# Which PSUM banks an output projection takes, and which engine scales its norms, in a one-core hybrid encoder layer

## The chip, the core and the metric

The kernel runs on one core of one Trainium2 chip. The metric is the device time of one execution in microseconds (us), lower is better. The kernel before took 1556.27 us in the median of three runs (1555.42 to 1558.12). One more execution was taken with the hardware profiler: it took 1553.82 us, of which 1551.8 us are the profiled span.

Five engines work side by side, each through its own list of instructions in order: TensorE (PE, matmuls and transposes, with its weight loads as PEld), VectorE (DVE), ScalarE (ACT), GpSimd (POOL), and SyncE (SP), which issues the DMAs. Matmuls write to PSUM, which this program uses as eight banks of 128x512 float32; DVE and ACT read results out of it, which is called eviction here.

## The reference

One encoder layer on 1024 tokens of width 1024: a mixer (windowed attention beside a gated delta rule) with an output projection, a cross-attention into 256 memory tokens with an output projection, and a SwiGLU feed-forward block. Each is normalised before and after:

```python
def _rms_norm(x, gain):
    y = xf * lax.rsqrt(jnp.mean(xf * xf, axis=-1, keepdims=True) + EPS)
    return y * gain

for l in range(DEPTH):
    ...
    mix = jnp.concatenate([attn_o, dn_o], axis=-1) @ w_out[l]
    x = x + _rms_norm(mix, g_mix_post[l])
    c = _memory_cross_attention(_rms_norm(x, g_cross_pre[l]), _rms_norm(mem, g_mem[l]),
                                w_cq[l], w_ckv[l], w_co[l])
    x = x + _rms_norm(c, g_cross_post[l])
    f = _swiglu(_rms_norm(x, g_ffn_pre[l]), w_gate_up[l], w_down[l])
    x = x + _rms_norm(f, g_ffn_post[l])

# inside the windowed attention, per head and block of 128 queries
denom = jnp.sum(p, axis=-1, keepdims=True) + jnp.exp(sk - m)
o = jnp.einsum('bnhgqk,bnkhd->bnqhgd', p / denom, vw)
```

## The kernel before

Every large product is made of three matmuls on operands split in a high and a low part: `split` (L103 and L104) casts the high part on ACT and subtracts the low part on DVE, or on POOL where the call says so. Weights come through `load_w` (L126): a DMA into `wraw`, then `whi` and `wlo`. Each of these three has two buffers, so the weights of a step can be made ready only when those of two steps earlier have been used.

The program is written in the order of the layer; a scheduler then interleaves the instructions on every engine, with data, buffers and banks as its limits. The stages the change touches, in the order of time:

- **Windows** (`window`, L643 to L690). Sixteen blocks of windowed attention, numbered 0 to 15. PE makes the scores (`psw`, L654), DVE masks them and takes the maximum (L656), ACT makes the exponentials (L663), and the four probability tiles are scaled by one over the sum (L671 to L674): by DVE for the first eight blocks, by ACT for the last eight. PE then transposes them (`ptw`, L680), they are split into `ph` and `pl`, and PE makes the output (`pow`, L685). The last blocks run beside the memory's value projection (`pcv`, L965).
- **Mixer projection** (`mid_gemm` with `w_out`). It works on 512 tokens at a time, here called the first and the second half, and on each in two chunks of 512 output columns. A chunk has four accumulators `pmg` (L1052), one per 128 tokens, and four weight steps; a step gives each accumulator six matmuls. So a chunk is 96 matmuls, and its first accumulator is complete 18 matmuls before its last. An eviction is a square with its sum on ACT (L1055) and a multiplication by the gain on DVE (L1056). Then each 128 tokens get: a reciprocal root on POOL (L1064, L1065), the residual on DVE (L1066), a store, a square on ACT (L1069), a second reciprocal root on POOL (L161, L162), and the scaling of the next norm into `xr` on DVE (L1072). PE turns `xr` (`ptn`).
- **Cross queries** (`cross_q`, `pcq`, L261), with the low parts of the weights made by POOL.
- **Cross-attention** (`cross_attention`). For each half four heads follow one another: 24 score matmuls (`pcs`, L1133), maximum on DVE, exponentials on ACT (L1140), sums and scaling on DVE, eight transposes (`pct`, L1149), their split into `cph` and `cpl`, 12 output matmuls (`pco`, L1159), whose result is split back into the query's tiles. `pcs` and `pco` share the pool `px` of two banks.
- **Cross projection**: `mid_gemm` with `w_co` on the first half, the transposes of its norm (`ptn`, L1190) with POOL making low parts, `mid_gemm` on the second half, and the start of the feed-forward block (`pA`, L1227).

In this part PSUM is three pools: `pg` with four banks, `pn` and `px` with two each. A pool hands out its banks in turn, in the order in which the program is written. The argument `banks` of `mid_gemm` says from which pool each accumulator of the first and of the second chunk comes. By default the second chunk takes its first two accumulators from `px` and its last two from `pg`. In the program `mid_gemm` on the first half of the cross projection stands behind all heads of both halves, so its turn in `px` comes after all of their tiles.

Of the kernel before, what the change touches and what calls it, by code (L numbers as in the profile page):

```python
# [13 lines left out]
AF = mybir.ActivationFunctionType  # L14
ALU = mybir.AluOpType
# [8 lines left out]
NT = S // P  # L24
# [52 lines left out]
def tile_hybrid_block(  # L77
# [6 lines left out]
    nc = tc.nc  # L84
    x, mem, out = x[0], mem[0], out[0]
    w_in, w_out, w_cq, w_ckv, w_co = w_in[0], w_out[0], w_cq[0], w_ckv[0], w_co[0]
# [100 lines left out]
    d_x1 = dram.tile([S, D], F32, name="d_x1")  # L187
    d_x2 = dram.tile([S, D], F32, name="d_x2")
# [443 lines left out]
    def window(n, g):  # L632

        tok = slice(n * P, (n + 1) * P)
        k0, k1 = max(n - 1, 0), min(n + 1, NT - 1) + 1
        nb = k1 - k0
        w = nb * P
        band = C[:, _AT["band0"] - C0 + (k0 - n + 1) * P:][:, 0:w]

        khi, klo = (t[:, k0 * P:k1 * P] for t in keys[g])  # L640
        qr = tw.tile([P, 4, P], F32, tag="qr", name="qr", bufs=1)
        for r in range(2):
            nc.sync.dma_start(qr[64 * r:64 * r + 64], d_q[256 * g:256 * g + 256, tok].rearrange("(h e) t -> e h t", h=4))  # L643
        qs = tw.tile([P, 4, P], F32R, tag="qs", name="qs")
        nc.scalar.copy(qs, qr)
        nc.gpsimd.tensor_tensor(qs[64:128], qr[64:128], f32(qs[64:128]), ALU.subtract)

        m4 = tw.tile([P, 4], F32, tag="m4", name="m4")
        ssum = tw.tile([P, 4], F32, tag="ssum", name="ssum")
        pr = []  # L650
        for hh in range(4):
            pp = pw.tile([P, 512], F32, tag="pw", name="psw")
            for i, kk in enumerate((khi, klo)):
                nc.tensor.matmul(pp[:, 0:w], qs[:, hh, :], kk, start=(i == 0), stop=(i == 1))  # L654
            sc = tw.tile([P, 384], F32, tag="sc", name="sc", bufs=8)
            nc.vector.tensor_tensor_reduce(out=sc[:, 0:w], in0=pp[:, 0:w], in1=band, scale=0.125,  # L656
                                           scalar=sink[:, 4 * g + hh:4 * g + hh + 1], op0=ALU.add, op1=ALU.max,
                                           accum_out=m4[:, hh:hh + 1])
            pr.append(sc)
        nm = tw.tile([P, 4], F32, tag="nm", name="nm")  # L660
        nc.vector.tensor_scalar(nm, m4, -1.0, None, ALU.mult)
        for hh in range(4):
            nc.scalar.activation(pr[hh][:, 0:w], pr[hh][:, 0:w], AF.Exp, bias=nm[:, hh:hh + 1],  # L663
                                 accum_out=ssum[:, hh:hh + 1])
        es = tw.tile([P, 4], F32, tag="es", name="es")
        nc.gpsimd.tensor_tensor(es, sink[:, 4 * g:4 * g + 4], m4, ALU.subtract)
        nc.scalar.activation(es, es, AF.Exp)
        nc.vector.tensor_tensor(es, es, ssum, ALU.add)
        nc.vector.reciprocal(es, es)
        for hh in range(4):  # L670
            if g * NT + n < 8:  # L671
                nc.vector.tensor_scalar(pr[hh][:, 0:w], pr[hh][:, 0:w], es[:, hh:hh + 1], None, ALU.mult)
            else:
                nc.scalar.mul(pr[hh][:, 0:w], pr[hh][:, 0:w], es[:, hh:hh + 1])  # L674
        yield
        po = pw.tile([P, 4, P], F32, tag="pow", name="pow", bufs=1)
        for j in range(nb):
            pp = pw.tile([P, 512], F32, tag="pw", name="ptw")
            for hh in range(4):
                nc.tensor.transpose(pp[:, hh * P:(hh + 1) * P], pr[hh][:, j * P:(j + 1) * P], ident)  # L680
            ph = tw.tile([P, 512], F32R, tag="ph", name="ph")
            pl = tw.tile([P, 512], F32R, tag="pl", name="pl")
            split(ph, pl, pp)
            for i, pe_ in enumerate((ph, pl)):
                nc.tensor.matmul(po.rearrange("p h t -> p (h t)"), vhl[:, k0 + j, g].rearrange("p r e -> p (r e)"), pe_,  # L685
                                 start=(j == 0 and i == 0), stop=(j == nb - 1 and i == 1))
        ao = tw.tile([P, 4, P], F32, tag="ao", name="ao", bufs=1)[0:64]
        nc.scalar.copy(ao, po[64:128])
        nc.vector.tensor_tensor(ao, po[0:64], ao, ALU.add)
        nc.sync.dma_start(d_mix[g * 256:(g + 1) * 256, tok].rearrange("(h e) t -> e h t", e=64), ao)  # L690
# [322 lines left out]
    def turn_norm(xn, gname, his, los, pin=False):  # L1013

        for k in range(KT):
            pt = pn.tile([P, 512], F32, tag="pn", name="ptn")
            for j in range(4):
                t = nc.tensor.transpose(pt[:, j * P:(j + 1) * P], xn[j][:, k * P:(k + 1) * P], ident)
                if pin and k + j == 0:
                    tc.keep_in_program_order(t)  # L1020
            split(his[:, k, :], los[:, k, :], pt, gain(gname, k))
# [9 lines left out]

    PG, PN, PX = (pg, "pg"), (pn, "pn"), (px, "px")

    def mid_gemm(tz, act, w, gp, res, dst, hf, between=None, banks=([PG] * 4, [PX] * 2 + [PG] * 2)):


        zs = [tz.tile([P, D], F32, tag="z", name="z", bufs=4) for _ in range(4)]
        sss = [tz.tile([P, 2], F32, tag="zss", name="zss", bufs=8) for _ in range(4)]
        for ch in range(2):
            cs = slice(ch * 512, (ch + 1) * 512)  # L1040
            if ch and between:
                between()

            pp = [q_.tile([P, 512], F32, tag=t_, name="pmg") for q_, t_ in banks[ch]]
            for kp in range(4):
                whi, wlo = load_w(w[kp * 256:(kp + 1) * 256, cs], 2, 512)
                for t in range(4):
                    tt = slice(t * P, (t + 1) * P)
                    for kk in range(2):
                        k = 2 * kp + kk  # L1050
                        for i, (w_, a) in enumerate(((whi, 0), (whi, 1), (wlo, 0))):
                            nc.tensor.matmul(pp[t], act[a][:, k, tt], w_[:, kk, :], start=(k == 0 and i == 0),  # L1052
                                             stop=(k == KT - 1 and i == 2))
            for t in range(4):
                nc.scalar.activation(zs[t][:, cs], pp[t], AF.Square, accum_out=sss[t][:, ch:ch + 1])  # L1055
                nc.vector.tensor_tensor(zs[t][:, cs], pp[t], gp[:, cs], ALU.mult)  # L1056
        xn = []
        for t in range(4):
            tok = slice(hf * HALF + t * P, hf * HALF + (t + 1) * P)
            z = zs[t]  # L1060
            xr = tz.tile([P, D], F32, tag="xr", name="xr", bufs=XR)
            nc.sync.dma_start(xr, res[tok, :])
            rs = tz.tile([P, 1], F32, tag="prs", name="prs", bufs=4)
            nc.gpsimd.tensor_scalar(rs, sss[t][:, 1:2], sss[t][:, 0:1], D * EPS, ALU.add, ALU.add)  # L1064
            nc.gpsimd.tensor_tensor(rs, rs, mhalf[:, 0:1], ALU.pow)  # L1065
            nc.vector.scalar_tensor_tensor(z, z, rs, xr, ALU.mult, ALU.add)  # L1066
            nc.sync.dma_start(dst[tok, :], z)
            s2 = tz.tile([P, 1], F32, tag="ps2", name="ps2", bufs=4)
            nc.scalar.activation(xr, z, AF.Square, accum_out=s2)  # L1069
            r2 = tz.tile([P, 1], F32, tag="pr2", name="pr2", bufs=4)  # L1070
            rstd_of(r2, s2, 1.0 / D, EPS)
            nc.vector.tensor_scalar(xr, z, r2, None, ALU.mult)  # L1072
            xn.append(xr)
        return xn

# [6 lines left out]
    tz = L1.enter_context(pool("tz", 1))  # L1082
    gp = gpost_tile(tz, g_mix_post)
    mxT = [operand(opA, "s0"), [opB_first[0], opB3.tile([P, KT, HALF], F32R, tag="b3", name="b3")]]
# [7 lines left out]
                              .rearrange("(k p) t -> p k t", p=P))  # L1092
            split(mxT[hf][0][:, k2, :], mxT[hf][1][:, k2, :], raw[:, k2, :])
    LR.close()
    xn0 = mid_gemm(tz, mxT[0], w_out, gp, x, d_x1, 0, banks=([PG] * 4, [PX] * 2 + [PN] * 2))
    h2T = [[opB.tile([P, KT, HALF], F32R, tag=b1, name=b1), opB_first[2]]]
    xn1 = mid_gemm(tz, mxT[1], w_out, gp, x, d_x1, 1, between=lambda: turn_norm(xn0, "cross", *h2T[0], pin=True))
    h2T.append(operand(opA, "s0"))
    turn_norm(xn1, "cross", *h2T[1])

# [64 lines left out]
    q1 = cross_q(1)  # L1165
# [10 lines left out]
    tz = L3.enter_context(pool("tz2", 1, side="right"))  # L1176
# [16 lines left out]
    for k in range(KT):  # L1193
        pt = turned_k(xn, k)
        nc.scalar.activation(raw[:, k, :], pt, AF.Identity, scale=gain("ffn", k))
        split(x1h[:, k, :], x1l[:, k, :], raw[:, k, :], eng=nc.gpsimd)
    xn = mid_gemm(tz, q1, w_co, gp, d_x1, d_x2, 1)
    T2, T4 = (blocks(t) for t in operand(opB, "s1"))
    T1, T3 = (blocks(t) for t in operand(opB, "s2"))
    for k in range(HK):  # L1200
# [355 lines left out]
```

## Time and profile before

| | |
|---|---|
| median of three runs | 1556.27 us |
| profiled execution | 1553.82 us |
| its span | 1551.8 us |
| PE busy | 1488.0 us (96%) |
| DVE busy | 1074.3 us (69%) |
| ACT busy | 740.3 us (48%) |
| POOL busy | 379.9 us (24%) |
| PE's share of the chain that ended last | 70% |

Places in time (us from the start of the span): the last windows run until about 572, the mixer projection from 552 to 647, the queries and the first half's heads from 647 on, the first half's cross projection begins at 762, the second half's heads end at 839, the second half's cross projection ends at 903, and the feed-forward block fills the rest.

In the rows of a timeline or of the chain the first number is the start, the second the duration, then engine, line, operation, output and inputs, and the count of merged instructions; in square brackets stands how long the engine sat idle before it, and who released it. Matmuls overlap one another, so the pace of a long merged row says more than the duration of one matmul.

### The profile page before, as it was taken

What the parts mean: (1) busy time and instruction counts of PE and PEld (TensorE: products, weight loads), DVE (VectorE), ACT (ScalarE), POOL (GpSimd) and SP (SyncE); (2) the same over time, 40 slices, a digit from 0 to 9 for tenths busy, and PEclk for the clock granted to TensorE, in tenths of its full rate; (3) what the DMA queues carried; (4) which work ended last, traced back from release to release, by engine and by line L of the source; (5) the groups of instructions that cost most, each with busy time, mean ns of one, the idle gap of its engine ahead of it and who ended that gap; (6) DMA issues with size and microseconds to landing.
All of it is one profiled execution on the core that took longest, in us unless ns stands there. A gap on an engine that the chain in (4) does not pass through costs nothing.

```text
span 1551.8 us, 21044 instructions
## 1 busy us (share of the span) xinstructions
PE 1488.0 (96%) x7451; PEld 1248.9 (80%) x7451; DVE 1074.3 (69%) x1728; ACT 740.3 (48%) x1522; POOL 379.9 (24%) x364
## 2 busy tenths in 40 slices
PE   6999999998999999999987999999999999999997
PEld 5888888787989788888876887888888888888786
DVE  6868999686888766643444577776867554696665
ACT  5578732557467764443333664332323332354532
POOL 2020210111256103433000531443433432000021
PEclk9999999999999999999999999999999999999999
DMA  6244575856996755542210554344433334853354
GB/s 205 75 117 136 158 189 158 190 173 187 328 303 210 246 196 180 179 155 77 68 41 27 188 192 144 116 128 129 156 118 113 105 106 150 290 188 98 102 175 164
DMA packets 264710, 242.95 MB, mean 157 GB/s; under 512 B 33800, under 2 KB 203677, under 8 KB 264605
## 3 DMA queue, kind: packets, MB, share of 16 engines
q1 hardware_dynamic: 264605, 241.62, 50.0%
q8 instruction: 58, 0.95, 0.3%
q14 instruction: 47, 0.39, 0.1%
HBM read 172.07 MB, written 66.88 MB: 154 GB/s over the span
## 4 chain that ended last, share of the span: by engine, by line
PE 70%; DVE 7%; DMA 5%; ACT 5%; issue 2%; SPq 1%; POOL 1%; DVEq 0%; POOLq 0%; ACTq 0%
PE pmg L1052 11%; PE pD L1227 8%; PE pE L1227 8%; PE pA L1227 7%; PE pdX L1417 6%; PE pcq L261 5%; PE pdA L1417 4%; PE pB L1227 4%; PE psc L809 3%; PE pg L261 3%; PE pdD L1417 2%; PE pco L1159 2%; PE pcs L1133 2%; PE pck L949 1%; PE pdX L1510 1%
## 5 line engine op out<-in xcount | busy, mean ns | idle before, releaser
L103 ACT CAST whi<-wraw 128x1024 fp32r<-128x1024 f32 x108 | 113.6, 1052 | 176.6 <-PE pmg L1052 50.1
L261 PE MATMUL pg<-hlo,whi 128*128 128x512 f32 x352 | 139.7, 397 | 0.0
L261 PE MATMUL pg<-hhi,whi 128*128 128x512 f32 x352 | 139.3, 396 | 0.0
L261 PE MATMUL pg<-hhi,wlo 128*128 128x512 f32 x352 | 138.8, 395 | 0.0
L104 POOL TENSOR_TENSOR wlo<-wraw,whi 128x1024 fp32r<-128x1024 f32 x38 | 92.5, 2435 | 184.1 <-ACT whi L103 176.6
L104 DVE TENSOR_TENSOR wlo<-wraw,whi 128x1024 fp32r<-128x1024 f32 x70 | 87.1, 1245 | 71.9 <-ACT whi L103 64.4
L1052 PE MATMUL pmg<-whi,b 128*128 128x512 f32 x384 | 117.0, 393 | 1.1 <-DVE b L104 0.9
L1227 PE MATMUL pA<-s,whi 128*128 128x512 f32 x352 | 109.3, 392 | 1.0 <-ACT m L1244 1.0
L1052 PEld LDWEIGHTS pmg<-whi,b 128*128 128x128 f32 x384 | 71.5, 188 | 16.3 <-DVE b L104 1.4
L261 PEld LDWEIGHTS pg<-hhi,whi 128*128 128x128 f32 x352 | 66.6, 189 | 13.6 <-ACT hhi L103 0.2
L1417 PE MATMUL pdX<-dhl,whi 128*128 128x512 f32 x264 | 76.0, 390 | 1.5 <-DVE zv L1472 0.7
L1227 PEld LDWEIGHTS pA<-s,whi 128*128 128x128 f32 x352 | 65.5, 188 | 14.7 <-ACT m L1244 1.5
L261 PEld LDWEIGHTS pg<-hhi,wlo 128*128 128x128 f32 x352 | 66.5, 189 | 13.0
L261 PEld LDWEIGHTS pg<-hlo,whi 128*128 128x128 f32 x352 | 66.5, 189 | 12.9
L1304 POOL TENSOR_TENSOR act<-act,up 128x512 f32<-128x512 f32 x33 | 50.1, 1519 | 87.6 <-DVE up L1303 47.3
L1052 PE MATMUL pmg<-wlo,b 128*128 128x512 f32 x192 | 71.1, 391 | 0.0
L103 ACT CAST whi<-araw 128x1024 fp32r<-128x1024 f32 (+1 forms) x36 | 35.4, 982 | 71.0 <-PE pdX L1417 27.6
L1227 PE MATMUL pA<-s,wlo 128*128 128x512 f32 x176 | 68.7, 391 | 0.0
L104 DVE TENSOR_TENSOR wlo<-araw,whi 128x1024 fp32r<-128x1024 f32 (+1 forms) x36 | 40.8, 1133 | 38.9 <-ACT whi L103 38.9
L286 DVE SCALAR_TENSOR_TENSOR acc<-cp,cols,acc 128x1024 f32<-128x1024 f32 x48 | 62.1, 1295 | 0.1
L1276 POOL TENSOR_TENSOR sr<-wraw 128x512 f32<-128x512 f32 x22 | 31.0, 1410 | 126.5 <-DMA wraw<-in_w_gate_up_dram 125.2
L1447 POOL TENSOR_SCALAR frs<-sq 128x1 f32<-128x1 f32 x8 | 12.0, 1498 | 195.9 <-ACT jk L1436 194.9
(414 smaller groups left out, 4107.8 us busy)
## 6 DMA issues: line engine op xcount, KB each, us to landing
wraw<-in_w_gate_up_dram SPq DMA_DIRECT2D x52, 512.0 KB, 3.8
kv<-d_kv SPq DMA_DIRECT2D x32, 512.0 KB, 6.7
wraw<-in_w_in_dram SPq DMA_DIRECT2D x22, 512.0 KB, 4.7
b<-in_w_down_dram SPq DMA_DIRECT2D x20, 512.0 KB, 6.9
araw<-d_as SPq DMA_DIRECT2D x20, 512.0 KB, 3.7
pz<-d_pz SPq DMA_DIRECT2D x32, 256.0 KB, 5.2
wraw<-in_w_ckv_dram SPq DMA_DIRECT2D x16, 512.0 KB, 9.2
wraw<-in_w_out_dram SPq DMA_DIRECT2D x16, 512.0 KB, 3.7
```

The lines of the kernel that those rows point to most:

```text
L103: nc.scalar.copy(hi, src)
L104: (eng or nc.vector).tensor_tensor(lo, src, f32(hi), ALU.subtract)
L261: nc.tensor.matmul(p_, w[:, k, :], ah[a][:, k, :], start=(k == 0 and i == 0), stop=(k == nk - 1 and i == 2))
L286: nc.vector.scalar_tensor_tensor(acc, cp[:, t:t + S], taps[t], acc, ALU.mult, ALU.add)
L809: nc.tensor.matmul(out[:, d, h, :], lt[:, d, h, :], rt[:, d, h, :], start=True, stop=True)
L1052: nc.tensor.matmul(pp[t], act[a][:, k, tt], w_[:, kk, :], start=(k == 0 and i == 0), stop=(k == KT - 1 and i == 2))
L1133: nc.tensor.matmul(pp[:, t2_, :], q[a][:, ct, tt], kr_[b_][:, ct, :], start=(j == 0 and i == 0), stop=(j == 1 and i == 2))
L1159: nc.tensor.matmul(po, vr_[a][:, kt, cs], pts[kt][b_], start=(kt == 0 and i == 0), stop=(kt == 1 and i == 2))
L1227: nc.tensor.matmul(out_, w[a][:, k, :], xx[b_][:, k, :], start=(start and k == 0 and i == 0), stop=(k == HK - 1 and i == 2), skip_group_ch ...
L1276: nc.gpsimd.tensor_tensor(s[0], b_[:, 0:HK], b_[:, HK:], ALU.add)
L1304: nc.gpsimd.tensor_tensor(o_, o_, up, ALU.mult)
L1417: nc.tensor.matmul(banks[t], a[:, k - k0, tt], w, start=(first and k == 0 and i == 0), stop=(k == NB - 1 and i == 2), skip_group_check=not ...
```

## The change

Three edits.

1. The default of `banks` becomes four accumulators from `pg` in both chunks. The two calls of the mixer projection name their banks, the same ones as before. So the two calls of the cross projection alone take other banks: `px` is out of their second chunk.
2. A new argument `vec` says which engine scales the norm. DVE does it, as before, in the mixer's first half and the cross projection's second half. In the mixer's second half and the cross projection's first half ACT does it, as an Identity activation with the reciprocal root as scale.
3. The windows' probabilities are scaled by DVE in blocks 0 to 7 and 13 to 15, by ACT in blocks 8 to 12.

```diff
-            if g * NT + n < 8:
+            if not 8 <= g * NT + n < 13:
                 nc.vector.tensor_scalar(pr[hh][:, 0:w], pr[hh][:, 0:w], es[:, hh:hh + 1], None, ALU.mult)
             else:
                 nc.scalar.mul(pr[hh][:, 0:w], pr[hh][:, 0:w], es[:, hh:hh + 1])
...
-    def mid_gemm(tz, act, w, gp, res, dst, hf, between=None, banks=([PG] * 4, [PX] * 2 + [PG] * 2)):
+    def mid_gemm(tz, act, w, gp, res, dst, hf, between=None, banks=([PG] * 4, [PG] * 4), vec=False):
...
-            nc.vector.tensor_scalar(xr, z, r2, None, ALU.mult)
+            if vec:
+                nc.vector.tensor_scalar(xr, z, r2, None, ALU.mult)
+            else:
+                nc.scalar.activation(xr, z, AF.Identity, scale=r2)
...
-    xn0 = mid_gemm(tz, mxT[0], w_out, gp, x, d_x1, 0, banks=([PG] * 4, [PX] * 2 + [PN] * 2))
+    xn0 = mid_gemm(tz, mxT[0], w_out, gp, x, d_x1, 0, banks=([PG] * 4, [PX] * 2 + [PN] * 2), vec=True)
...
-    xn1 = mid_gemm(tz, mxT[1], w_out, gp, x, d_x1, 1, between=lambda: turn_norm(xn0, "cross", *h2T[0], pin=True))
+    xn1 = mid_gemm(tz, mxT[1], w_out, gp, x, d_x1, 1, banks=([PG] * 4, [PX] * 2 + [PG] * 2),
+                   between=lambda: turn_norm(xn0, "cross", *h2T[0], pin=True))
...
-    xn = mid_gemm(tz, q1, w_co, gp, d_x1, d_x2, 1)
+    xn = mid_gemm(tz, q1, w_co, gp, d_x1, d_x2, 1, vec=True)
```

Lines after L1072 move by up to four in the changed kernel: `pcs` is L1137 there, `pct` L1153, `pco` L1163.

The scheduler answers with another order. On PE, in the second head of the second half, this stood before (`kr` and `vr` are the memory's keys and values, `b_7540` and `b_7541` the second half's query tiles, into which the heads' results go back):

```order
L1133 MATMUL pcs<-kr_6142,b_7540 128x256
L1149 MATMUL pct<-ident,cpr 128x128 x8
L1159 MATMUL pco<-cph,vr_6143 128x512 x2
L1159 MATMUL pco<-cpl,vr_6143 128x512
L1159 MATMUL pco<-cph,vr_6144 128x512
```

The last score matmul, the transposes and the outputs followed one another, with nothing else between, and so in the third and the fourth head. In the changed kernel PE has this at the second head's outputs (`b_6962` and `b_6963` are the first half's query tiles):

```order
L1052 MATMUL pmg<-wlo,b_6962 128x512
L1052 MATMUL pmg<-whi,b_7540 128x512
L1052 MATMUL pmg<-whi,b_7541 128x512
L1052 MATMUL pmg<-wlo,b_7540 128x512
L1052 MATMUL pmg<-whi,b_7540 128x512
L1052 MATMUL pmg<-whi,b_7541 128x512
L1163 MATMUL pco<-cph,vr_6143 128x512 x2
L1052 MATMUL pmg<-wlo,b_7540 128x512
L1163 MATMUL pco<-cpl,vr_6143 128x512
L1163 MATMUL pco<-cph,vr_6144 128x512
```

Projection matmuls moved in among the heads, those of the first half and then of the second. In that head 32 of them stand between scores and transposes, 21 between transposes and outputs, 22 behind the outputs. In the third head it is 1 between the two halves of the scores, 19 ahead of the transposes, none between transposes and outputs and 4 behind. In the fourth head 10 stand between the halves of the scores, 10 ahead of the transposes and none between transposes and outputs; then follow four transposes of the first half's norm and 120 projection matmuls mixed with the other transposes. From the end of the second half's projection on PE's order is that of before.

On ACT, from the casts of the second head's results to the fourth head's exponentials, this stood before:

```order
L103 CAST b_7540<-pco 128x512 x2
L1140 ACTIVATE cpr,csum<-pcs,cmx 128x256 x4
L103 CAST cph<-pct 128x512 x2
L103 CAST b_7540<-pco 128x512 x2
L1140 ACTIVATE cpr,csum<-pcs,cmx 128x256 x4
```

The changed kernel has, from the casts of the second head's results on:

```order
L103 CAST b_7540<-pco 128x512 x2
L1075 ACTIVATE xr<-z,pr_8429 128x1024
L1075 ACTIVATE xr<-z,pr_8442 128x1024
L1069 ACTIVATE xr,ps_8453<-z 128x1024
L103 CAST whi<-wraw 128x1024
L1075 ACTIVATE xr<-z,pr_8455 128x1024
L1144 ACTIVATE cpr,csum<-pcs,cmx 128x256 x4
L103 CAST whi<-wraw 128x1024
L103 CAST cph<-pct 128x512 x2
```

Three scalings, a square and a weight cast of the projection moved ahead of the third head's exponentials.

On DVE, in the norm of the mixer's second half (the `pr` are the reciprocal roots, `b_6963` the low part of a query):

```order
 L1056 TENSOR_TENSOR z<-pmg,gpost 128x512
-L1072 TENSOR_SCALAR xr<-z,pr_6845 128x1024
 L1066 SCALAR_TENSOR_TENSOR z<-z,prs,xr 128x1024
-L1072 TENSOR_SCALAR xr<-z,pr_6858 128x1024
-L1072 TENSOR_SCALAR xr<-z,pr_6871 128x1024
-L104 TENSOR_TENSOR b_6963<-pcq,b_6962 128x512
-L1072 TENSOR_SCALAR xr<-z,pr_6884 128x1024
-L104 TENSOR_TENSOR b_6963<-pcq,b_6962 128x512
+L104 TENSOR_TENSOR b_6963<-pcq,b_6962 128x512 x3
```

The four scalings left DVE; they stand on ACT now, between its squares and weight casts.

## The prediction

> **What bounds the kernel now.** The page comes first: how much of the span has PE at work.
>
> ```profile
> span 1551.8 us, 21044 instructions
> ## 1 busy us (share of the span) xinstructions
> PE 1488.0 (96%) x7451; PEld 1248.9 (80%) x7451; DVE 1074.3 (69%) x1728; ACT 740.3 (48%) x1522; POOL 379.9 (24%) x364
> ```
>
> PE is busy for 96%, and the change takes no matmul away. So it can gain only where PE stands still or is stretched, 64 us at least. The next view is the table of windows, 10 us each; its columns are the window, its length, the busy us of PE, PEld, DVE, ACT and POOL with their counts, PE's granted clock, the DMA share and GB/s.
>
> ```profile
> 790.00:800.00 10.00, 10.00 (x49) 8.22 (x48) 6.62 (x11) 5.36 (x15) 0.00 (x0) 1.00 0.14 52
> 800.00:810.00 10.00, 6.34 (x39) 4.93 (x39) 4.89 (x11) 4.11 (x12) 0.00 (x0) 0.94 0.00 0
> 810.00:820.00 10.00, 7.39 (x40) 6.02 (x39) 4.55 (x10) 3.19 (x11) 0.00 (x0) 0.89 0.01 2
> 820.00:830.00 10.00, 7.80 (x37) 5.82 (x36) 3.92 (x7) 2.15 (x4) 0.00 (x0) 0.83 0.00 0
> 830.00:840.00 10.00, 6.12 (x31) 4.19 (x30) 5.31 (x12) 4.19 (x12) 0.00 (x0) 1.00 0.00 0
> 840.00:850.00 10.00, 10.00 (x46) 8.28 (x45) 2.45 (x2) 2.11 (x2) 0.00 (x0) 1.00 0.24 82
> ```
>
> From 800 to 840 no engine is full, DMA rests, and PE's clock drops with its idleness. The chain that ended last, in order of time, shows what runs there (a row is a merged piece of the chain).
>
> ```profile
> 712.13 2.79 PE pco L1159 x12
> ...
> 766.52 2.87 PE pcs L1133 x24
> 769.39 6.60 PE pmg L1052 x29
> 776.87 3.64 PE pmg L1052 x16
> ...
> 802.31 3.14 PE pcs L1133 x24
> 809.64 3.79 PE pco L1159 x10
> 814.81 3.14 PE pcs L1133 x24
> 822.15 4.24 PE pco L1159 x10
> 827.77 3.15 PE pcs L1133 x24
> 839.38 26.80 PE pmg L1052 x117
> ```
>
> These are the second half's second, third and fourth head, each waiting for itself: scores, maximum, exponentials, transposes, outputs, split. Earlier heads had query or projection matmuls between their steps; these have none. Two banks explain it. Projection chunk two has its first two accumulators in `px`, whose turn comes after the last head, so only its other two could go ahead; with two weight buffers that stops after two steps. The rest of the projection waits until 839.38.
>
> **Edit 1, the banks.** PE's own timeline gives the end of the first head's outputs, and the steps of the fourth head.
>
> ```profile
> 800.98 0.40 PE L1159 MATMUL pco<-cph,vr 128*128 128x512 f32 x1
> ...
> 834.03 0.63 PE L1149 MATMUL pct<-ident,cpr 128*128 128x128 f32 x4 [0.80 <-DVE cpr L1143]
> ...
> 838.04 0.40 PE L1159 MATMUL pco<-cph,vr 128*128 128x512 f32 x1
> ```
>
> The stretch runs from 800.98 + 0.40 = 801.38 to 839.38, 38.0 us. Where PE had cover, a head cost 2.87 (24 scores), 776.87 - 769.39 - 6.60 = 0.88 (eight transposes) and 2.79 (12 outputs), 6.54 us; three heads cost 19.6. So 18.4 us are PE time in which projection matmuls could run, at 26.80 / 117 = 0.229 us each. In the new order they do. What stays, by the counts of the order:
>
> - The second head has 32, 21 and 22 of them behind its three steps, 7.3, 4.8 and 5.0 us. A filled step of before had 6.60 us and less. Nothing is left there.
> - The third and fourth head have nothing between transposes and outputs. In the trace this pair took 838.44 - 834.03 = 4.41 us for 0.44 + 2.79 of work: 1.2 left in each, 2.4.
> - The fourth head has ten (2.3 us) ahead of its transposes. Unfilled, the second transposes came 834.03 - (827.77 + 3.15) = 3.1 us after the scores: 0.8 left.
> - Behind the last outputs the projection reads the head just made. That took 839.38 - 838.44 = 0.94 us; four transposes now cover 0.44 of it, 0.5 left. Behind the third head four matmuls read it too, but its first column block first: I take 0.5 again.
> - ACT has five passes of 1.06 us (a row below) ahead of the third head's exponentials, 5.3 us, and a POOL reciprocal root to wait for; PE has 22 projection and 24 score matmuls, 7.9 us, over it. I take 1.0, between 0 and 2.5 (one POOL step of 1.47 and one pass more).
>
> Together 5.2 us left, a gain of 13.2. The bounds: 16.0 if only the 2.4 is left; 9.1 if the fourth head, the least covered, kept its whole excess of 839.38 - 827.77 - 6.54 = 5.1, with 1.2, 0.5 and 2.5 for the rest.
>
> Do four banks cost more elsewhere? The rows of the two eviction lines, and of two ACT and POOL operations (count, then minimum, median and maximum in ns):
>
> ```profile
> L1055 ACT ACTIVATE z<-pmg x32: 581/598/623, 574.5 to 903.9; 128x512 f32<-128x512 f32 x32
> L1056 DVE TENSOR_TENSOR z<-pmg,gpost x32: 676/692/693, 575.2 to 906.1; 128x512 f32<-128x512 f32 x32
> L1027 ACT ACTIVATE gpost<-gpost x3: 1059/1059/1065, 526.7 to 1349.9; 128x1024 f32<-128x1024 f32 x3
> 862.20 1.47 POOL L162 TENSOR_TENSOR pr<-pr,mhalf 128x1 f32<-128x1 f32 x1
> ```
>
> A bank comes round after 96 matmuls and its accumulator is complete 18 matmuls, 4.1 us, before the next chunk needs it; its eviction is 0.60 + 0.69 = 1.3 us. I cost the three changes at nothing: 2.8 us of matmuls hide them. If an eviction stood in a queue that long, each would cost up to 1.3. [...]
>
> The projection's weight loads and stores move forward on SP with it, one load now behind three stores instead of two. They fall into windows with a DMA share of 0.00 and 0.01: nothing.
>
> **Edit 2, the norms.** In the list of waits and the row of the scaling:
>
> ```profile
> PE ptn L1018 <- DVE xr L1072: 2.5, 2, 1.5
> ...
> PE psw L654 <- DVE m L656: 1.4, 2, 1.0
> PE pow L685 <- DVE pl L104: 1.3, 2, 0.9
> L1072 DVE TENSOR_SCALAR xr<-z,pr x16: 747/754/2949, 604.9 to 913.8; 128x1024 f32<-128x1024 f32 x16
> 657.12 2.37 POOL L104 TENSOR_TENSOR wlo<-wraw,whi 128x1024 fp32r<-128x1024 f32 x1
> 657.18 2.86 DVE L1072 TENSOR_SCALAR xr<-z,pr 128x1024 f32<-128x1024 f32 x1 [0.44 <-POOL pr L162]
> ```
>
> In the mixer's second half two scalings started beside a POOL split and took 2.9 us in place of 0.75; PE waited for both, 2.5 us. On ACT they take 1.06. What is late next is that split itself, which ends at 657.12 + 2.37 = 659.5. PE's longest wait, 1.5, ended with the scaling at 660.0, so it began at 658.5, and up to 1.0 of it stays; I take 0.8 and a gain of 1.7, between 2.5 and a loss of 1.1 (a weight cast behind one ACT pass). [...]
>
> In the cross projection's first half the scaling costs ACT 4.2 us, counted above, and relieves DVE of 3.0 off the path. Its second half is as before, and so are the 36 `pA` matmuls ahead of its transposes: nothing.
>
> **Edit 3, the windows.** Twelve scalings change engines:
>
> ```profile
> L674 ACT ACTIVATE sc<-sc,es x32: 494/602/621, 451.5 to 557.5; 128x384 f32<-128x384 f32 x24, 128x256 f32<-128x256 f32 x8
> L672 DVE TENSOR_SCALAR sc<-sc,es x32: 344/414/421, 308.5 to 430.9; 128x384 f32<-128x384 f32 x24, 128x256 f32<-128x256 f32 x8
> ```
>
> ACT loses 8 x 0.602 + 4 x 0.494 = 6.8 us, DVE gets 8 x 0.414 + 4 x 0.344 = 4.7. Around these blocks PE waited 1.4 and 1.3 us for DVE, which itself was behind ACT. Bounds: both waits go, a gain of 2.7; or four scalings (1.7 us) stand ahead of a maximum or a `pl` that PE wants, a loss of 1.7. I take a gain of 1.0, since the order on PE otherwise holds the same work.
>
> **The sum.** 13.2 + 1.7 + 1.0 = 15.9 us. The profiled execution took 1553.82: 1537.9 for such a one. Against the median of 1556.27, 2.45 above it, the forecast is 1540.4. All good ends give 16.0 + 2.5 + 2.7 = 21.2 and 1535.1; all bad ones 9.1 - 1.1 - 1.7 = 6.3 and 1550.0.
>
> **The rivals.** *Half the cover.* The weights of the projection arrive too late, or its matmuls are used up, after the second head. Then only that head's excess, 814.81 - 802.31 - 6.54 = 6.0, and the 0.9 ahead of it are won: 1549.4. For it speaks that two weight buffers already stopped the projection once; against it that DMA is idle there and ACT half empty. Chance 0.10.
>
> *Full cover.* Nothing is left in the heads and both other edits reach their best: 18.4 + 2.5 + 2.7 = 23.6, 1532.7. Against it stand the third and fourth head's bare steps. Chance 0.06.
>
> *ScalarE in the way.* ACT works in order, and every norm it scales waits there for POOL: square 1.06, root 1.47, scaling 1.06, at least 3.6 us; eight of them 28.7. If nothing ran beneath them, the exponentials and casts behind would hold PE for as long: 1556.3 - 18.4 + 28.7 = 1566.6, slower. It turns slower once more than 18.4 / 28.7, two thirds, is bare. The order speaks against it, with evictions and casts between these steps. Chance 0.03.
>
> *No effect.* The two banks were not what held the projection, and PE still stands from 801 to 839: 1556. The order, with projection matmuls among the heads, speaks against it. Chance 0.02.
>
> **How the numbers follow.** The forecast has the remaining 0.79. The range goes from 1535, all good ends, to 1550, all bad ends, which takes in the half cover; full cover, the slow case and no effect, 0.11, are outside. A measurement of this kernel tells about 0.2%, 3.1 us, from no change. Forecast, half and full cover are faster by more: 0.95. No effect is within: 0.02. ScalarE in the way is slower: 0.03.
>
> **What would show it.** In the profile of the changed kernel, windows between the first head's outputs and the projection should have PE near 10 of 10 for the second head and a clock of 1.00; PE's waits there should be by `cpr`, `cph` and `b` in the third and fourth head, some 5 us in all; the wait of `ptn` for `xr` should be under 1 us; waits of `pmg` for evictions should be absent. The prediction is wrong if the three heads still take over 30 us without projection matmuls between them, if `pmg` waits for L1055 or L1056, or if exponentials start late behind L1075 in every head.

## The result, and the profile after

The changed kernel takes 1539.61 us in the median of four runs (1538.95 to 1540.86), the kernel before 1555.85 beside it (1552.12 to 1558.12): a ratio of 0.9899, with a 95% interval of 0.9878 to 0.992. The forecast was 1540.4, between 1535 and 1550. The profiled execution took 1539.27 us, of which 1537.6 are its span; by the working of the prediction it would have been 1537.9. Two terms of the sum were too small and one had the wrong sign.

First the head of the page, as before: the span, and each engine's busy time.

```profile
span 1537.6 us, 21036 instructions
PE 1481.4 (96%) x7451; PEld 1246.6 (81%) x7451; DVE 1067.1 (69%) x1732; ACT 743.3 (48%) x1518; POOL 374.6 (24%) x364
```

The 7451 matmuls are the same, and the share is 96% again; shares of the whole span say nothing here. The table of windows for the changed kernel, with the columns as before:

```profile
800.00:810.00 10.00, 10.00 (x56) 8.64 (x55) 4.29 (x5) 3.28 (x4) 0.00 (x0) 1.00 0.12 35
...
820.00:830.00 10.00, 10.00 (x45) 8.18 (x44) 9.42 (x12) 9.21 (x18) 8.22 (x12) 1.00 0.64 239
830.00:840.00 10.00, 9.62 (x58) 8.31 (x56) 4.78 (x10) 7.16 (x16) 0.74 (x2) 1.00 0.31 110
840.00:850.00 10.00, 9.01 (x46) 7.19 (x47) 5.06 (x9) 2.67 (x8) 0.00 (x0) 1.00 0.15 53
850.00:860.00 10.00, 8.98 (x48) 6.96 (x47) 5.14 (x9) 4.76 (x11) 0.00 (x0) 1.00 0.18 53
```

Where 31 to 40 matmuls and transposes ran in ten us, 45 to 58 run now, and the granted clock is 1.00 throughout. ACT, DVE and POOL do the projection's evictions, norms and weight splits in the same windows.

To see where the time went, both traces are cut at four points that lie on PE in every version: the end of the scan's last transposes (`psc`, L901), the first query matmul (`pcq`), the end of the last one, and the first matmul of the feed-forward block (`pA`). These are the rows of PE's timeline at the cuts, first of the kernel before, then of the changed one:

```profile
514.63 0.66 PE L901 MATMUL psc<-ident,ol 128*128 128x128 f32 x4 [0.28 <-DVE ol L896]
...
646.54 0.62 PE L261 MATMUL pcq<-b,whi 128*128 128x512 f32 x2
...
757.17 0.39 PE L261 MATMUL pcq<-s,wlo 128*128 128x512 f32 x1
...
902.95 0.62 PE L1227 MATMUL pA<-s,whi 128*128 128x512 f32 x2
```

```profile
515.91 0.66 PE L901 MATMUL psc<-ident,ol 128*128 128x128 f32 x4 [1.24 <-DVE ol L896]
...
650.02 0.61 PE L261 MATMUL pcq<-b,whi 128*128 128x512 f32 x2
...
757.76 0.39 PE L261 MATMUL pcq<-s,wlo 128*128 128x512 f32 x1
...
889.16 0.62 PE L1231 MATMUL pA<-s,whi 128*128 128x512 f32 x2
```

| stretch | edit in it | before, us | after, us | difference |
|---|---|---|---|---|
| start to the scan's end | none | 515.3 | 516.6 | +1.3 |
| scan's end to first query | 3 | 131.3 | 133.5 | +2.2 |
| first to last query | 2 | 111.0 | 108.1 | -2.9 |
| last query to feed-forward | 1, and half of 2 | 145.4 | 131.0 | -14.4 |
| feed-forward | none | 648.9 | 648.4 | -0.4 |

The first row is no effect: the order of PE's instructions up to the end of the scan is the same in both. So a row of this table from one execution may be off by as much, and each had to be tried alone.

### The profile page after: what moved, and what is told of

The parts are those of the page before. It is cut to its first block, busy times and chain, and to the rows that moved or that the text cites. A ratio compares the mean times of both kernels' runs of the same rounds, so it can differ in the third digit from the quotient of the medians.

```text
span 1537.6 us, 21036 instructions
## 1 busy us (share of the span) xinstructions
PE 1481.4 (96%) x7451; PEld 1246.6 (81%) x7451; DVE 1067.1 (69%) x1732; ACT 743.3 (48%) x1518; POOL 374.6 (24%) x364
## 5 line engine op out<-in xcount | busy, mean ns | idle before, releaser
L1052 PEld LDWEIGHTS pmg<-whi,b 128*128 128x128 f32 x384 | 71.4, 188 | 15.3 <-ACT b L103 1.3
```

## The experiments

Times are medians, with the ratio to the kernel before measured on the same chip (1555.02, 1554.87 and 1556.08 us for the first, second and third four). This is the same cut for every version; the last column is the feed-forward block.

| version | time, us | ratio (95%) | scan's end at | to first query | queries | to feed-forward | rest |
|---|---|---|---|---|---|---|---|
| e1_banks | 1539.0 | 0.9891 (0.9868 to 0.9913) | 517.3 | 131.6 | 110.8 | 131.06 | 647.7 |
| e2_norms | 1552.89 | 0.998 (0.9966 to 0.9994) | 515.4 | 132.1 | 108.14 | 150.9 | 648.2 |
| e3_windows | 1555.22 | 1.0001 (0.9985 to 1.0016) | 515.9 | 132.9 | 110.7 | 145.5 | 647.7 |
| e4_no_windows | 1537.26 | 0.9882 (0.9859 to 0.9904) | 515.3 | 132.9 | 108.13 | 131.04 | 647.4 |
| e5_one_px | 1553.71 | 0.9992 (0.9975 to 1.0009) | 518.5 | 131.2 | 108.13 | 146.3 | 648.1 |
| e6_first_only | 1536.67 | 0.9878 (0.986 to 0.9896) | 515.1 | 131.2 | 108.13 | 130.94 | 647.8 |
| e7_mixer_four | 1537.35 | 0.9883 (0.9866 to 0.99) | 516.3 | 131.9 | 108.13 | 131.01 | 647.5 |
| e8_all_scalar | 1539.66 | 0.9899 (0.9875 to 0.9923) | 520.8 | 131.1 | 108.13 | 131.04 | 650.6 |
| e9_changed_again | 1539.23 | 0.9898 (0.9882 to 0.9915) | 515.2 | 133.8 | 108.13 | 131.04 | 648.1 |
| e10_block15 | 1534.92 | 0.9872 (0.9857 to 0.9887) | 516.8 | 132.3 | 108.13 | 131.04 | 647.6 |
| e11_all_vector | 1535.89 | 0.9875 (0.9858 to 0.9892) | 515.2 | 131.0 | 108.13 | 131.03 | 647.8 |
| e12_low_last | 1534.64 | 0.9871 (0.9853 to 0.9888) | 517.0 | 131.1 | 108.11 | 130.27 | 647.7 |

### Each edit alone, and the third left out

The first version keeps edit 1 and undoes the others:

```diff
-            if not 8 <= g * NT + n < 13:
+            if g * NT + n < 8:
...
-            if vec:
+            if True:
```

> Edit 1 alone: four banks from pg in both chunks of the cross projection, the norms and windows as before. Theory A (the two traces laid side by side: the banks won 14.4 us, the norms 2.9, the windows lost 3.5, and the three add up): about 14 us under the kernel before, 1541.5 against 1555.9. The prediction's terms (13.2): 1542.7. Rival B (the banks need the ScalarE scaling of the first half's norms, because VectorE then has no time for the splits of the heads): under 10 us won, over 1546, with PE waiting longer for cpl or cph in the third and fourth head.

Theory A held: 16.0 us under the kernel before by the medians, 14.3 by the stretch. The stretch to the feed-forward block is 131.06 without the ScalarE scaling and 131.04 with it (e4), so rival B fell: the banks need nothing of edit 2.

The second keeps edit 2, with the old default of `banks` and the old windows:

```diff
-banks=([PG] * 4, [PG] * 4), vec=False):
+banks=([PG] * 4, [PX] * 2 + [PG] * 2), vec=False):
```

> Edit 2 alone: ScalarE scales the norms of the mixer's second half and of the cross projection's first half. Theory A: 2.9 us won in the mixer's second half, and no ptn that waits for xr: about 1553. The prediction's term: 1.7 won, 1554.2. Rival (the 2.9 of the traces came from the mixer's later start, because its loads and casts had other neighbours, not from the scaling): nothing won, 1556, with VectorE passes of over 2 us still there beside a POOL split.

2.1 us by the medians, and 2.7 in the queries' stretch: 108.14 in place of 110.7 to 111.0. Theory A held. But its next stretch took 150.9 us, not 145.4. Windows of this kernel in the bare heads:

```profile
820.00:830.00 10.00, 8.71 (x36) 6.89 (x37) 3.33 (x6) 2.25 (x4) 0.00 (x0) 0.68 0.00 0
830.00:840.00 10.00, 7.27 (x26) 5.49 (x25) 3.86 (x10) 3.24 (x11) 0.00 (x0) 0.66 0.00 0
```

The granted clock was 0.68 and 0.66 here, where the execution of before shows 0.83 and 1.00. PE's waits in this stretch come to 12.7 us, against 12.6 in the kernel before, so nearly all of the 5.5 us is in the pace of the work and not in waits. The granted clock is the figure that differs; that it accounts for the whole is not shown.

The third keeps edit 3 alone.

> Edit 3 alone: VectorE scales the probabilities of blocks 13 to 15. Theory A (its new order delays the last casts and stores of the windows): 3.5 us slower than before, 1559.4, with PE waiting for whi and wlo at pcv and at the first pmg. The prediction's term: 1.0 won, 1554.9. Rival C (the 3.5 us are chance of one execution, or come from the other edits): within 1 us of before.

The edits of the two versions above undo the rest. By the medians it is 0.2 us slower, with an interval from 2.3 us faster to 2.5 slower: theory A's 3.5 is outside, the forecast's gain of 1.0 inside, and so is a loss of nearly 2. The stretch took 132.9, against 131.3 in the execution of before.

The fourth is the changed kernel with the old condition, `if g * NT + n < 8:`.

> The changed kernel without edit 3 (ScalarE scales blocks 8 to 15 as before). Theory A: the changed kernel less the 3.5 us, so 1536 where it took 1539.6, 1 to 1.5 percent under the kernel before; the first pmg of the mixer's second half starts near 599.4 instead of 602.9. The prediction's term for the windows (a gain of 1.0): 1540.6. Rival C: as the changed kernel, 1539.6.

1537.26, between theory A and the prediction's term. The edits add up: 16.0 and 2.1 alone are 18.1, together 17.8. Its stretch to the first query was 132.9 without edit 3, though, the longest of those without it. From 530 to 550 its granted clock was 0.83, where the others without edit 3 had 0.91 or 1.00. So two executions could not settle theory A's 3.5, of which 1.3 stand ahead of the windows that edit 3 changes.

### The banks

One of the four accumulators goes back to `px`:

```diff
-banks=([PG] * 4, [PG] * 4), vec=False):
+banks=([PG] * 4, [PX] + [PG] * 3), vec=False):
```

> The changed kernel without edit 3, and with the first accumulator of the second chunk back in px, in both calls of the cross projection: one bank instead of two. Theory (the turn in px holds the whole projection: an accumulator there waits for all heads, and with two weight buffers the other three stop after two weight steps): the three bare heads are back, the stretch from the queries' end to the feed-forward's start is some 145 us instead of 131.0, and the time is 1537.3 + 14 = 1551. Rival (each accumulator out of px brings its share): three quarters of the 14.4 stay, 3.6 us are lost, 1541.

The theory held: one bank loses all of it. PE's waits from the last query to the feed-forward block in this kernel (the columns are the total, the number and the longest):

```profile
PE pct L1153 <- ACT cpr L1144: 5.0, 3, 1.7
PE pct L1153 <- DVE cpr L1147: 2.4, 3, 0.8
PE pcs L1137 <- DVE b L104: 1.9, 2, 0.9
...
PE ptn L1194 <- ACT xr L1075: 0.6, 1, 0.6
PE pmg L1052 <- ACT whi L103: 0.5, 1, 0.5
```

The transposes of three heads wait again for exponentials and scaling. The number of projection matmuls that ran ahead of the bare heads shows where the projection stops: 120 in the kernel before and 132 here. That is the 96 of the first chunk and two weight steps of six matmuls for each accumulator outside `px`, two of them before and three here.

The two lower rows are new. They stand in e2 as well, whose banks are those of before: without projection matmuls spread over the heads, the norm's scaling on ScalarE lies bare. The stretch is 146.3 in place of 145.4. So edit 2 costs up to 0.9 us where edit 1 is missing; a share of that can be the one bank in which this version differs from the kernel before.

Next, only the first half's call keeps four banks:

```diff
-    xn = mid_gemm(tz, q1, w_co, gp, d_x1, d_x2, 1, vec=True)
+    xn = mid_gemm(tz, q1, w_co, gp, d_x1, d_x2, 1, banks=([PG] * 4, [PX] * 2 + [PG] * 2), vec=True)
```

> The changed kernel without edit 3, four banks from pg in the second chunk for the first half's cross projection alone; the second half's takes px again, as before. Theory (only the first half's call stands in front of running heads; when the second half's second chunk begins the heads are done): as with both, 131 us for that stretch and 1537 us, within 1. Rival (the second half's projection covers the fourth head as well): up to the fourth head's 5.1 us lost, 1542.

130.94 and 1536.67: the whole gain comes from the first half's call, as the theory had it. Then the opposite, four banks also for both calls of the mixer:

```diff
-    xn0 = mid_gemm(tz, mxT[0], w_out, gp, x, d_x1, 0, banks=([PG] * 4, [PX] * 2 + [PN] * 2), vec=True)
+    xn0 = mid_gemm(tz, mxT[0], w_out, gp, x, d_x1, 0, vec=True)
```

> The changed kernel without edit 3, and with the mixer's two projections on four banks too, in both chunks. It measures what a chunk costs that takes the banks of the chunk before it, three times more. The prediction's reading (an eviction of 1.3 us lies beneath 18 matmuls, 4.1 us): nothing, 1537.3, and no pmg that waits for L1055 or L1056. [...]

1537.35 in place of 1537.26, and the list of PE's waits is empty from 550 to 760. The stretch to the first query is 131.9, within the 131.1 to 132.9 of the versions with the old banks there. Three more changes on the same four banks cost nothing that shows.

### The norms

> The changed kernel without edit 3, and with all four norms scaled by ScalarE, also the mixer's first half and the cross projection's second half, where POOL makes no weight split beside them. Theory (VectorE is only slow beside a POOL split, elsewhere the choice is worth nothing): 1537.3, within 1; the stretches from the mixer's second half to the queries and from there to their end as before. Rival (ScalarE has the evictions' squares and the weight casts to do there, and 1.06 us in place of 0.75 for each scaling): PE waits for z or whi, up to 8 times 0.3, 2.4 us slower, 1539.7.

The edit is `if False:` for `if vec:` at L1072. 1539.66, as the rival had it, and at another place than it named: the mixer's stretch is 131.1, among the shortest, while the feed-forward block takes 650.6, longer than in any other version here. PE's waits at its beginning, from 891 to 960, in this kernel:

```profile
PE pA L1231 <- ACT m L1248: 1.3, 2, 0.7
PE pA L1231 <- DVE wlo L104: 1.1, 2, 0.5
```

In the version without edit 3 (e4) `pA` waits only 1.0, for `m`. The 1.1 for `wlo` is new, and 0.3 more is for `m`. With those of `pB` and `pD` the waits of that window are 3.9 us against 2.7. The granted clock was also 0.91 from 931 to 951, where e4 had 1.00 throughout that part, from 887 to 967. How much of the 3 us is the clock's isn't shown, and the intervals of the two medians overlap. So VectorE in the cross projection's second half is the better choice or no worse, which is as far as this goes.

### The windows

The changed kernel itself ran again, beside three others.

> The changed kernel itself once more, beside a kernel with edit 3 for block 15 alone, one for all blocks, and one without edit 3, on the same chip. So far edit 3 alone measured 0.2 us over the kernel before, on top of the other two 2.4 over the kernel without it, and its stretch (end of the scan to the first query) took 132.9 and 133.5 us where eight executions without it took 131.1 to 132.9, 131.7 in the mean. Theory D (edit 3 costs some 1.5 us: PE waits for two weight casts at pcv): 1539, and 133 us for that stretch, with pcv waiting for whi. Rival C (it costs nothing, the differences are chance): 1537.3 and 131.7 us.

1539.23 and 133.8: Theory D's numbers. On the same chip the version without edit 3 (e12, below) took 1534.64, 4.6 us less, of which 0.8 is its own further change. Over all traces the stretch took 132.9, 133.5 and 133.8 us with edit 3 (mean 133.4), and 131.1 to 132.9 in the nine executions where the windows are as before (mean 131.6). So the edit costs some 1.8 us by the stretch; the medians leave it anywhere between 0.2 (e3) and 3.8. PE's waits between 516 and 603 in the changed kernel:

```profile
PE pcv L965 <- ACT whi L103: 2.9, 2, 1.6
PE psc L901 <- DVE ol L896: 1.2, 1, 1.2
PE pcv L965 <- DVE wlo L104: 1.1, 2, 0.6
PE pow L685 <- DVE pl L104: 0.9, 1, 0.9
PE pmg L1052 <- ACT whi L103: 0.9, 1, 0.9
```

And in the kernel before:

```profile
PE psw L654 <- DVE m L656: 1.0, 1, 1.0
PE pow L685 <- DVE pl L104: 0.9, 1, 0.9
PE pow L685 <- ACT ph L103: 0.6, 1, 0.6
PE pcv L965 <- DVE wlo L104: 0.2, 1, 0.2
```

The wait for the mask and maximum (`m`) went, as forecast, and the 0.9 for `pl` stayed; in place of the first PE waits for weights of the memory's values, 2.9 us for casts and 1.1 for low parts. The longer of the two waits for casts, 1.6 us, ended with this one of the changed kernel:

```profile
536.37 1.04 ACT L103 CAST whi<-wraw 128x1024 fp32r<-128x1024 f32 x1 [0.62 <-DMA wraw<-in_w_ckv_dram]
```

It waited for its weights to be loaded, and it ended 20.8 us after the scan's end, about when the same cast of the kernel before did, after 21.1. PE came to it sooner, because it no longer waited for `m`, and waited there instead. The cast of the other wait does come later. ScalarE's timeline shows it, first in the kernel before, then in the changed one:

```profile
540.64 1.05 ACT L103 CAST whi<-wraw 128x1024 fp32r<-128x1024 f32 x1
541.59 0.62 ACT L663 ACTIVATE sc<-sc,nm 128x384 f32<-128x384 f32 x1
```

```profile
543.24 0.60 ACT L663 ACTIVATE sc<-sc,nm 128x384 f32<-128x384 f32 x1
543.84 1.03 ACT L103 CAST whi<-wraw 128x1024 fp32r<-128x1024 f32 x1
```

Before, the cast stood ahead of the block's four exponentials; now it stands behind them, 3.2 us later, or 1.9 if both are counted from the scan's end.

Is it that order? Two versions tell. In the first, VectorE takes block 15 alone, and the cast stands ahead again:

```diff
-            if not 8 <= g * NT + n < 13:
+            if not 8 <= g * NT + n < 15:
```

> The changed kernel with edit 3 for block 15 alone: ScalarE scales blocks 8 to 14. In its order the weight cast for pcv stands ahead of the exponentials of block 14 again, as before. Theory D (the loss is the order around blocks 13 and 14): no pcv that waits for whi, 131.7 us for the stretch, 1537.3. Rival (the last scaling on VectorE delays the last output and store): the wait of pmg for whi behind the last store is there, 133 us, 1539.

1534.92, 132.3 us, and a wait for `whi` at `pcv` of 0.3, as in e1, e7 and e12 where the windows are as before; no `pmg` waits for `whi`. So there is no loss, as Theory D has it, within what the stretch scatters by. In the second, VectorE takes all sixteen (`if True:`).

> The changed kernel with edit 3 for all sixteen blocks: VectorE scales them all. Theory D (the order around block 13 costs, not VectorE's load): as the changed kernel, 1539, 133 us from the scan's end to the first query, and the same start. Rival E (VectorE bounds the time of blocks 8 to 12, where it is busy for 75 to 95 percent): 20 scalings of 0.41 us more, 8 us of VectorE work, of which PE gets 3 or more to wait; the scan ends 3 us or more later, 1541 to 1546.

Both failed. VectorE did bear 7 us more between 440 and 515, as this window shows in the version with edit 3 everywhere and then in the one without it:

```profile
440.00:515.00 75.00, 69.93 (x553) 66.38 (x552) 69.55 (x183) 44.92 (x150) 43.39 (x56) 1.00 0.71 221
```

```profile
440.00:515.00 75.00, 69.06 (x550) 65.96 (x549) 62.59 (x161) 55.21 (x170) 41.78 (x56) 1.00 0.72 220
```

69.55 us in place of 62.59, and the scan ended at 515.2 all the same, so Rival E fell; and the stretch took 131.0, not Theory D's 133. PE's waits between 516 and 603 with all sixteen on VectorE:

```profile
PE pcv L965 <- ACT whi L103: 3.1, 1, 3.1
PE pcv L965 <- DVE wlo L104: 0.2, 1, 0.2
```

Here too PE waits for a cast, 3.1 us, which itself waited for its load, and for next to nothing else: 3.3 in all, against 2.7 in the kernel before and 5.8 in the changed one (without its `psc` row, which is the scan's). So the wait for that cast alone is not the price.

The sum of the waits follows the stretch only beside the granted clock, since e9, the same kernel as the changed one, has waits of 4.0 us and the longest stretch. From 530 to 550 that clock was 1.00 in the changed kernel's first execution and in e3, with waits of 5.8 and 5.5 us and stretches of 133.5 and 132.9. It was 1.00 too in four executions without edit 3 (e1, e7, e8, e12), with 3.9 to 4.3 us and 131.1 to 131.9; e10, with 4.6 us and 132.3 at 1.00, lies between. It was 0.83 in e9, and in e4 without edit 3, which had 3.7 us of waits and 132.9. So at a like clock edit 3 costs 1.7 us, nearly all of it in waits, or 0.8 in the one pair at 0.83. Why three blocks come out worse than one or sixteen was not settled.

### What is left over in the heads

The last version turns the six matmuls of `pco` so that those that read the low part come last; the same products are summed in another order:

```diff
-                for kt in range(2):
-                    for i, (a, b_) in enumerate(((0, 0), (0, 1), (1, 0))):
-                        nc.tensor.matmul(po, vr_[a][:, kt, cs], pts[kt][b_], start=(kt == 0 and i == 0),
-                                         stop=(kt == 1 and i == 2))
+                for i, (kt, a, b_) in enumerate(((0, 0, 0), (0, 1, 0), (1, 0, 0), (1, 1, 0), (0, 0, 1), (1, 0, 1))):
+                    nc.tensor.matmul(po, vr_[a][:, kt, cs], pts[kt][b_], start=(i == 0), stop=(i == 5))
```

> The changed kernel without edit 3, and with the six matmuls of each pco in another order: the four that read cph first, the two that read cpl last. It tests what is left over in the third and fourth head, where PE waits 0.8 us for cpl and 1.0 for cph behind the transposes. Theory (VectorE's subtraction comes after ScalarE's cast, so the low parts are what is late): 0.8 won, 130.2 us from the end of the queries to the feed-forward block in place of 131.0, the wait for cpl gone, 1536.5. Rival (the wait moves on to the second cph or to b): 131.0 as before, 1537.3.

The stretch took 130.27, 0.77 less, in place of 130.94 to 131.06 in the others with edit 1. PE's timeline at the third head's outputs in this kernel:

```profile
838.43 2.12 PE L1162 MATMUL pco<-cph,vr 128*128 128x512 f32 x8 [0.52 <-ACT cph L103]
840.39 1.10 PE L1162 MATMUL pco<-cpl,vr 128*128 128x512 f32 x4
841.93 1.20 PE L1052 MATMUL pmg<-whi,b 128*128 128x512 f32 x4 [0.44 <-ACT b L103]
```

Eight matmuls on the high parts cover VectorE's subtraction; the wait for `cpl` is gone. In the stretch the waits for `b` grew from 0.4 to 0.9 us, as the rival had it, and it is shorter all the same. It is the fastest median, 1534.64, which beats the kernel before with a ratio of 0.9871 (0.9853 to 0.9888). It does not differ from block 15 alone (1534.92) by what these measurements can tell; the two together weren't tried.

## Why the prediction was right, point by point

**What bounds it.** Right: the three bare heads, 801 to 839, were the place. The cause given, a turn in `px` that comes after the last head, is shown by e5, where one such accumulator brings all three back, and by e6, where only the first half's call matters. That the free accumulators stop after two weight steps is borne out by the counts, 120 projection matmuls before and 132 in e5.

**Edit 1, the banks: 13.2 forecast, 14.4 measured.** The mechanism was right, and what is left over is 18.4 - 14.4 = 4.0 us, not 5.2. Its places, in PE's timeline of the changed kernel at the third and the fourth head:

```profile
838.59 1.04 PE L1153 MATMUL pct<-ident,cpr 128*128 128x128 f32 x8
...
840.14 0.74 PE L1163 MATMUL pco<-cph,vr 128*128 128x512 f32 x2 [0.52 <-ACT cph L103]
841.51 0.50 PE L1163 MATMUL pco<-cpl,vr 128*128 128x512 f32 x1 [0.63 <-DVE cpl L104]
...
844.32 1.19 PE L1052 MATMUL pmg<-whi,b 128*128 128x512 f32 x4 [0.22 <-ACT b L103]
...
852.81 0.60 PE L1153 MATMUL pct<-ident,cpr 128*128 128x128 f32 x4
853.79 0.63 PE L1153 MATMUL pct<-ident,cpr 128*128 128x128 f32 x4 [0.39 <-DVE cpr L1147]
854.88 0.72 PE L1163 MATMUL pco<-cph,vr 128*128 128x512 f32 x2 [0.46 <-ACT cph L103]
855.78 0.50 PE L1163 MATMUL pco<-cpl,vr 128*128 128x512 f32 x1 [0.18 <-DVE cpl L104]
...
858.42 0.39 PE L1163 MATMUL pco<-cph,vr 128*128 128x512 f32 x1
```

The third head takes 844.32 - 838.59 = 5.73 us from its transposes to the next matmul, for 0.88 + 2.79 of work: 2.1 left, where 1.2 + 0.5 was forecast. The fourth takes 858.81 - 852.81 = 6.0, of which 0.44 are four transposes of the norm: 1.9 left, where 0.8 + 1.2 + 0.5 was. Together 4.0, all that is left over; 4.2 was forecast for it. The term that was mis-sized is the 1.0 for five passes of ScalarE ahead of the third head's exponentials: with the norms on VectorE (e1) the stretch is 131.06, with them on ScalarE 131.04, so it is nothing. The 22 projection and 24 score matmuls did cover the passes. The prediction also looked for some 5 us of waits in these two heads; PE's waits are by `cpr`, `cph` and `b`, as it said, and by `cpl`, but 2.6 us in all. The rest of the 4.0 shows in no wait.

That the bank changes cost nothing was right: e7 took 1537.35 with three more of them, where e4 took 1537.26, and from 550 to 910 no `pmg` of e7 waits for an eviction.

**Edit 2, the norms: 1.7 forecast, 2.7 measured** (the stretch took 108.11 to 108.14 us in all eleven executions with it, 110.72 to 111.02 in the three without). The step that failed is that 0.8 stays, because PE waits for POOL's weight split once the scaling is gone. It does not. Windows of the stretch, the kernel before and then the changed one:

```profile
650.00:660.00 10.00, 8.63 (x41) 6.93 (x39) 8.70 (x7) 4.49 (x9) 9.40 (x11) 1.00 0.88 318
660.00:670.00 10.00, 8.88 (x45) 7.21 (x46) 6.29 (x7) 3.98 (x6) 4.88 (x4) 1.00 0.36 108
```

```profile
650.00:660.00 10.00, 10.00 (x46) 8.27 (x45) 8.16 (x7) 7.82 (x13) 9.46 (x11) 1.00 1.00 346
660.00:670.00 10.00, 10.00 (x53) 8.33 (x52) 1.84 (x4) 7.60 (x11) 6.30 (x5) 1.00 0.57 185
```

PE is full in both windows now, and it waits for nothing from the first to the last query, so no wait for the split took the place of the wait for the scaling. The 2.5 us of waits went whole. Without edit 2 the stretch less its waits is 108.5 us in all three executions (waits of 2.5, 2.2 and 2.2), with it 108.1; these last 0.4 show in no wait, and their cause stays open. In the kernel before, the two scalings that ran beside a POOL split took 2.86 and 2.95 us and the other fourteen 0.75 to 0.79, while those two splits were not slowed themselves, at 2.37 and 2.39 us where the later ones took 2.40. The 2.7 measured is nearer to the 2.5 of PE's two waits, the prediction's upper bound, than to its 1.7. The cover named for the other half of edit 2 was right, and e5 puts its price without it at up to 0.9 us.

**Edit 3, the windows: a gain of 1.0 forecast, a loss of about 1.8 measured** in the stretch. It lies outside the bound of -1.7 by a little, within what the stretch scatters. The step that failed is "since the order on PE otherwise holds the same work": the wait for `m` went as forecast, but PE then stood before a weight cast that ended about when it did before, and the scheduler put the next cast behind exponentials. At a granted clock of 1.00 PE's waits are 5.8 and 5.5 us, where they are 3.9 to 4.3 without the edit. Only rows of the operations that change engine were priced, not those that get another neighbour.

**The sum.** 14.4 + 2.7 - 1.8 = 15.3, where 15.9 was forecast: errors of +1.2, +1.0 and -2.8 cancelled, so that the sum came out within 0.6 us is luck. The medians differ by 16.2, the profiled executions by 14.6.

**The rivals.** Half the cover (1549.4) did not happen: the weights arrived, and the second head is full. Full cover (1532.7) fell short by the two heads' 4.0 us. ScalarE was not in the way, by e1 against e4. No effect is what e5 looks like.

## What to carry to other kernels

A buffer or bank that is handed out in program order can hold back work that is written later, far beyond its own share (one accumulator of four in `px` made the stretch 146.3 us in place of 131.0): look for a stretch where no engine is full, and ask whose turn the idle work is waiting for, before adding speed. What an edit of engines costs is not only its own instructions; read in the new order which casts and loads got another neighbour, and measure such an edit alone, since a sum that comes out right can hide a term of the wrong sign. A stretch cut at the same two instructions resolved tenths where PE was full in it (108.11 to 108.14 us) or waited in the same way each time (130.94 to 131.06); where the waits and the granted clock changed from execution to execution, it resolved one or two us (131.1 to 132.9 in the nine executions with the windows as before).

## What the runs showed of the hardware

- PE's granted clock was below 1.00 in the bare heads: 0.83 to 0.94 in three windows of the execution before, 0.66 to 0.84 in all four of e2, 0.83 in two of e5. The longest single wait of PE there was 1.7 us, in the execution before and in e5. The prediction has the clock drop with PE's idleness; window by window it did not: the emptiest one, from 830 to 840 before, with PE busy for 6.12 of 10 us, had 1.00. Nor is it the same each time: from 530 to 550 the changed kernel had 1.00 in one execution and 0.83 in another (e9). With the heads filled, from 800 to 860 in the changed kernel, the clock was 1.00. That may be why the medians gain 16.0 in e1 and the stretch 14.3; neither this nor what makes the clock fall is shown.
- The stretch from the first query to the last, with PE full in it, repeated to 0.03 us (108.11 to 108.14 in eleven executions), while the end of the scan lay anywhere between 515.1 and 520.8 us in fourteen, and the stretch from there to the first query, in which PE waits for 2.7 us in the kernel before, took 131.1 to 132.9 us in the nine with the windows as before.
